# Decode rows and decode values as float32 matmuls on four column groups, and the 32-to-64 step of the inverse on packed odd columns, in one hybrid decoder layer

## The chip, the cores and the metric

The kernel runs on one core of a Trainium2 chip. A core has TensorE (PE, with its weight loads listed apart as PEld), VectorE (DVE), ScalarE (ACT), GpSimd (POOL) and SyncE (SP), which here issues all DMAs. The metric is device microseconds of one execution.

## The reference, cut to what matters

One layer serves 2048 prompt rows and 8 decode rows (one new token for each of 8 sequences) with the same weights: a mixer (a width-31 convolution module beside a gated DeltaNet with 4 heads), memory cross-attention, and a SwiGLU FFN.

```python
def gated_delta_chunked(q, k, v, g, beta, s0):        # chunks; per chunk:
    lower = jnp.where(strict, einsum(kb, k) * decay, 0.0)
    a_mat = lower + jnp.eye(c)
    u = triangular_solve(a_mat, v * beta[..., None])  # the kernel forms the inverse of a_mat
    w = triangular_solve(a_mat, kb * exp(gc)[..., None])

def memory_attend(h, mem_k, mem_v, w_mq, w_mo):
    q = (h @ w_mq).reshape(bsz, seq, MEM_HEADS, MEM_HD)
    pr = softmax(einsum('blhd,bmhd->bhlm', q, mem_k) * MEM_HD ** -0.5)
    o = einsum('bhlm,bmhd->blhd', pr, mem_v)
    return o.reshape(bsz, seq, MEM_HEADS * MEM_HD) @ w_mo

def decoder_layer(x, ...):
    x = x + parallel_mixer(rms_norm(x, norm_mix), ...)
    x = x + memory_attend(rms_norm(x, norm_mem_q), mem_k, mem_v, w_mq, w_mo)
    x = x + swiglu(rms_norm(x, norm_ffn), w_gate, w_up, w_down)
```

The decode rows have their own keys and values in a cache: 8 x 256 tokens x 1024 numbers each.

## The kernel before, in words

The prompt is cut into four blocks of 512 columns (TB). Big products use float32r operands, each split into a high part (ScalarE, rounded) and a low part (VectorE or GpSimd, the remainder); a product is then three matmuls: high x high, low x high, high x low (`three`). A float32 operand needs no split, but one call on it leaves two matmul records in the trace.

The program is written as one main line, which feeds TensorE, and many lanes (generators) that the main line advances by `tick`; a lane waits with `yield` for a tile, for room in a pool, for a PSUM bank, or for a time. Everything goes on a tape, and `Tape.order` then lists the instructions of each engine: it walks a model of the five engines, takes the ready instruction that stood earliest on the tape, and gives out tile buffers as it goes. So a change of durations or buffers anywhere places instructions anew behind it.

**The decode rows in the attention.** In the FFN of block 0, from f = 13, the main line takes the 16 row tiles of w_mq one after the other, two for each f; in the FFN of block 1, from f = 12, those of w_mo (`DEC_Q`, `DEC_O`, steps "dec" of `ffn_steps` and `ffn_steps_ds`). `dec_row` multiplies the 8 decode columns, as high and low parts side by side (16 columns of weights, tile hd_mix), by the high and the low part of a row tile of 128x512: two float32r matmuls into the tile dr. After eight tiles dr is copied, and the two halves are added by a matmul with the constant sel2 (tiles dq, dx).

Between the two lies the lane `dec_attend`: scores with the cached keys on VectorE, a softmax, and then the values. For each of two halves of the columns it loads 16 tiles of 128x512 (vtd; 8 sequences, 2 halves of the tokens), splits each (vth on ScalarE, vtl on VectorE), and multiplies by the packed probabilities (pb, 64 columns: 8 sequences x high and low x 4 heads) into the tile podd. `podt` is its transpose. The first row of w_mo needs the whole lane: there the main line calls `S.finish(dec_lanes["a"])`.

**The inverse.** `dn_front` runs 16 times (4 heads, 4 blocks) beside the projections, the attention products and the first FFN. A 128x128 matrix is inverted from 16x16 blocks upward, four matrices (NT) at a time: on the levels 16 and 32 a first product (pu from Tm with weights lo or lt), a mask (nms), a second product (pu from u1 with weights W), and a transpose of the inverse so far (ptw), copied to W. On level 16 the weights of the first product are the odd 16-blocks of lt, packed to 64 columns (lo), and W holds 64 rows. On level 32 they are the whole of lt and W. The last level, 64, is the same before and after.

Of the kernel before, what the change touches and what calls it, by code (L numbers as in the profile page):

```python
# [8 lines left out]
F32 = mybir.dt.float32  # L9
# [53 lines left out]
HOLD = 3  # L63
RES = 5
# [85 lines left out]
class Tape:  # L150
# [28 lines left out]
    def cost(self, eng, op, args, kw, outs, ins):  # L179
# [3 lines left out]
        if eng == "pe":  # L183
            m = elems(args[1])
            n = elems(args[2])
            if op == "transpose":
                return max(n, m) * 0.835 + 3, False, None
            if args[1].dtype == F32:
                return 2 * (max(max(m, 64) * 0.835, 2 * n * 0.4492) + 3), False, None
            return max(max(m, 64) * 0.835, (n if n >= 256 else 4 * n) * 0.4492) + 3, False, None  # L190
# [406 lines left out]
def hybrid_step(ctx: ExitStack, tc: tile.TileContext, i: dict, o: list):  # L597
# [23 lines left out]

    def transpose(out, in_, identity):
# [162 lines left out]
    def ffn_steps(b):  # L785
# [5 lines left out]
        for f in range(NF):  # L791
# [5 lines left out]
            dec = [w for w, (db, f0) in (("w_mq", DEC_Q), ("w_mo", DEC_O)) if db == b and f0 <= f < f0 + KC]  # L797
            steps += [("P5", f), ("P6", f)]
            steps += [("dec", dec[0], 2 * (f - (DEC_Q if dec[0] == "w_mq" else DEC_O)[1]) + n) for n in range(2) if dec]
            steps += [("Q2", f), ("Q3", f), ("Q7", f)]  # L800
            early = g is None and f + 1 < NF
# [5 lines left out]
            if g is not None:  # L807
                steps += [("down", g, j) for j in range(1, KC // 2)]
        if not hold and b != NB - 1:
            steps += [("down", NG - 1, j) for j in range(KC // 2)]  # L810
        return steps

    def ffn_steps_ds(b):
        steps = []
        for f in range(NF):
            if f == 0 or not early:
                steps.append(("Q1", f))
            dec = [w for w, (db, f0) in (("w_mq", DEC_Q), ("w_mo", DEC_O)) if db == b and f0 <= f < f0 + KC]
            steps += [("P5", f), ("P6", f)]
            steps += [("dec", dec[0], 2 * (f - (DEC_Q if dec[0] == "w_mq" else DEC_O)[1]) + n) for n in range(2) if dec]  # L820
# [6 lines left out]
            early = not units[0] + units[1] and f + 1 < NF  # L827
            if early:
                steps.append(("Q1", f + 1))
            steps += units[0] + [("P4", f)] + units[1]  # L830
# [26 lines left out]
    def ffn_plan(b):  # L857
        at = {}
        for st, f, *j in ffn_steps(b):
# [4 lines left out]
            elif st == "dec":  # L864
                plan.append((f, "r", j[0] % KC, j[0] // KC * TB))
# [85 lines left out]
    class WS:  # L951
# [60 lines left out]
        def split(self):  # L1012
            j = self.sp
            k = plan.raw_of[j]
            t = wpool.tile([P, 2, TB], F32R, tag="w", name=nm("w"))
# [6 lines left out]
            r = self.raw[k]  # L1022
# [296 lines left out]
    hd_mix = const("hd_mix", [P, KC, 16], F32R)  # L1319
# [7 lines left out]
    def dec_start():  # L1327
        dma(xd, i["xsT"])
        yield xd
        yield from dec_norm("norm_mix", hdn)  # L1330
        dec_split(hdn, hd_mix)
# [4 lines left out]
        for kc in range(KC):  # L1336
            mm(pb_, hd_mix[:, kc, 0:DEC], wbd[:, kc, :], kc == 0, False)
            mm(pb_, hd_mix[:, kc, DEC:16], wbd[:, kc, :], False, kc == KC - 1)
        V.tensor_copy(out=bd_dec, in_=pb_)
# [266 lines left out]
    def conv_block(b):  # L1606
# [4 lines left out]
        for t in range(NT):  # L1611
            sl = slice(b * TB + t * P, b * TB + (t + 1) * P)
            yield ("t2", 3 + RES)
# [22 lines left out]
            y = t2("lny", (P, 4, P))  # L1636
            for ct in range(4):
                A.activation(
                    out=y[:, ct, :], in_=pt[:, ct * P : (ct + 1) * P], func=AF.Silu, scale=vcol("conv_ln_g", ct),
                    bias=vcol("conv_ln_b", ct),  # L1640
                )
            dma(catc[:, :, sl].rearrange("c p t -> p c t"), y)
            drop(xi, x, y)
# [96 lines left out]

    def dn_front(h, b, sc, prev, out):
# [70 lines left out]
        dma(z_full(zl[z]), lt)  # L1812
        x16 = small("x16", [32, 272])
        w16 = small("w16", [32, 272], bufs=1)
# [11 lines left out]

        yield from base_inverse(x16, w16, bit)
# [6 lines left out]
        drop(bit, du)  # L1834
        W = t2("W", (64, NT, P))
# [7 lines left out]

        lo = small("lo", [P, NT, 64], bufs=1)
# [4 lines left out]
        for s in LEV[:-1]:  # L1849
            n = nms[s].shape[0]  # L1850
            yield ("ps", "s")
            pu = ps("pu1", shape=(n, NT, 64))
            for c in range(NT):
                mm(pu[:, c, :], (lo if n == 64 else lt)[:, c, :], left(Tm, s)[:, c], True, True)
            V.tensor_tensor(out=u1[:n], in0=pu, in1=bc(nms[s], 1, [n, NT, 64]), op=ALU.mult)
# [3 lines left out]
            for c in range(NT):  # L1859
                mm(pu[:, c, :], W[:, c, :], u1[:n, c, :], True, True)  # L1860
# [7 lines left out]
            W = t2("W", (P, NT, P))  # L1868
            A.activation(out=W, in_=pt, func=AF.Copy)
            yield W  # L1870

        yield ("ps", "s")
# [164 lines left out]
    for s, n_ in ((16, 64), (32, P)):  # L2037
        m = const(f"nms{s}", [n_, 64])
        GS.memset(m, -1.0)
        nb, w_ = 64 // s, n_ // 64 * s  # L2040
        GS.affine_select(out=m, in_=m, compare_op=ALU.is_ge, fill=0.0, base=s - w_, pattern=[[-w_, nb], [0, s]], channel_multiplier=1)
        GS.affine_select(out=m, in_=m, compare_op=ALU.is_ge, fill=0.0, base=w_ - 1, pattern=[[w_, nb], [0, s]], channel_multiplier=-1)
# [271 lines left out]
    def square_gemm(w, src, order, xs, done, dec, apart):  # L2314
# [10 lines left out]
        for m in range(n0):  # L2325
            if m == n0 - 1:
                S.until(lambda: any(C.bank_free(t) < 1e12 for t in ("mm", *others())), "fourth bank")
            pts.append([pm("rg", (P, hi - lo), others() if len(spans) * m + k > 2 else []) for k, (lo, hi) in enumerate(spans)])
# [27 lines left out]
    sel2 = const("sel2", [16, DEC])  # L2356
    V.tensor_tensor(out=sel2, in0=ident[:16, 0:DEC], in1=ident[:16, DEC:16], op=ALU.add)

    def dec_row(w, n, hd, then, at=[]):

        hf, kc = n // KC, n % KC
        if kc == 0:
            S.until(lambda: not any(c[0] is not None for c in convs) and C.bank_free("cv") < 1e12, "bank")
            at[:] = [ps("dr", "cv", (16, TB))]
        wt = ws.get(w, "r", kc, hf * TB)
# [3 lines left out]
        ws.free(1)  # L2369
        if kc == KC - 1:  # L2370
# [700 lines left out]
```

## Time and profile before

| | us |
|---|---|
| median of three runs | 2953.32 |
| lowest, highest | 2949.38, 2954.25 |
| profiled execution, span from first to last instruction | 2954.1 |
| mean granted TensorE clock | 0.995 |

The time of the profiled execution around its span isn't shown; the span lies within the three runs. By the first and last starts of their tiles, the input projections run to 711 us with the convolution and DeltaNet beside them and after them, the memory keys and values follow from 711, and the FFN of block 0 starts at 1175. The fronts end at 1452; the rows of w_mq stand from 1435 to 1562, the values from 1732 to 1947, the rows of w_mo from 1950 to 2052.

In the profile a row of a group gives line, engine, operation, tiles written<-read, sizes, count, then busy time, mean duration in ns, and idle time of the engine before it with what ended it. Nearly all instructions have line 474, a helper, so groups are told by their tiles. In the timeline, runs of like matmuls are merged to one row with a count; a bracket at its end is the idle time before it.

### The profile page before, as it was taken

The page shows a single profiled execution, that of the slowest core. Times are in us where ns is not written, and L with a number is a line of the kernel's source. Part 1 is how long each engine was busy: PE and PEld are TensorE (multiplying, and loading weights), DVE is VectorE, ACT ScalarE, POOL GpSimd, SP SyncE. Part 2 cuts the span into 40 slices and gives each one's busy share as a digit, 9 for nine tenths or more (in the row PEclk, how much of TensorE's full clock was granted, in tenths as well). Part 3 has the DMA queues.
Part 4 walks back from the last instruction along what each step waited for, and adds up shares of the span by engine and source line. Part 5 has one row for each costly group of instructions (what it writes and reads, how often), then busy time and mean ns, then how long its engine had stood idle before and what let it go on. Part 6 is the DMA issues. An engine that isn't in the chain of part 4 may idle for free.

```text
span 2954.1 us, 56406 instructions
## 1 busy us (share of the span) xinstructions
PE 2905.5 (98%) x19620; PEld 2619.1 (89%) x19620; DVE 2192.2 (74%) x4335; ACT 1486.5 (50%) x3093; POOL 1834.7 (62%) x1935
## 2 busy tenths in 40 slices
PE   9999999999999999999999999999999999999998
PEld 7999878887788888898988889989889999999998
DVE  8757888989655937977788976777865666776666
ACT  7544555555664545545554454444544444444444
POOL 4554454786546455558785138868514888758887
PEclk9999999999999999999999999999999999999999
DMA  6533335777673425755777677786627666666763
GB/s 215 154 101 111 125 106 166 239 255 239 203 257 110 144 86 186 224 184 184 257 241 257 221 239 221 227 257 217 195 86 228 205 207 181 211 230 194 215 207 124
DMA packets 363037, 569.44 MB, mean 193 GB/s; under 512 B 55840, under 2 KB 158560, under 8 KB 362736
## 3 DMA queue, kind: packets, MB, share of 16 engines
q1 hardware_dynamic: 362752, 565.84, 60.3%
q8 instruction: 155, 2.54, 0.4%
q14 instruction: 130, 1.06, 0.1%
HBM read 457.77 MB, written 108.51 MB: 192 GB/s over the span
## 4 chain that ended last, share of the span: by engine, by line
PE 85%; DVE 6%; DMA 4%; ACT 2%; POOL 2%; issue 1%; SPq 0%; POOLq 0%; DVEq 0%; ACTq 0%
PE fy L474 12%; PE rg L474 11%; PE hd L474 9%; PE fz L474 8%; PE fx L474 8%; PE sc L474 6%; PE dn L474 6%; PE dx L474 5%; PE dz L474 3%; PE glub L474 3%; PE glua L474 3%; PE pu L474 2%; DMA w<-sums 1%; DVE cacc L474 1%; PE dy L474 1%
## 5 line engine op out<-in xcount | busy, mean ns | idle before, releaser
L474 POOL TENSOR_TENSOR w<-raw,w 128x512 fp32r<-128x512 f32 (+1 forms) x777 | 1040.7, 1349 | 569.6 <-ACT w L474 514.3
L474 ACT ACTIVATE w<-raw 128x512 fp32r<-128x512 f32 (+1 forms) x1098 | 666.4, 619 | 900.0 <-PE rg L474 99.7
L474 PE MATMUL fy<-op,w 128*128 128x256 f32 (+1 forms) x3168 | 439.1, 283 | 4.2 <-DVE ffs L474 1.5
L474 PEld LDWEIGHTS fy<-op,w 128*128 128x128 f32 x3168 | 402.6, 189 | 9.7 <-DVE ffs L474 2.6
L474 PE MATMUL hd<-hT,w 128*128 128x512 f32 (+2 forms) x1920 | 395.8, 356 | 1.0 <-ACT w L474 0.6
L474 DVE SCALAR_TENSOR_TENSOR cacc<-cu,cw,cacc 128x512 f32<-128x512 f32 x480 | 359.2, 748 | 16.5 <-ACT cacc L474 9.7
L474 DVE TENSOR_TENSOR w<-raw,w 128x512 fp32r<-128x512 f32 (+1 forms) x321 | 287.5, 900 | 89.1 <-ACT w L474 86.4
L474 PEld LDWEIGHTS hd<-hT,w 128*128 128x128 f32 x1920 | 302.2, 188 | 45.4 <-ACT w L474 1.4
L474 PE MATMUL fx<-op,w 128*128 128x256 f32 (+1 forms) x2112 | 296.0, 284 | 6.6 <-ACT ffs L474 4.8
L474 PE MATMUL fz<-op,w 128*128 128x256 f32 (+1 forms) x2112 | 291.2, 283 | 2.9 <-DMA w<-sums 2.5
L474 POOL TENSOR_TENSOR sqj<-sqj,sqj 128x512 f32<-128x512 f32 (+1 forms) x98 | 134.1, 1368 | 251.8 <-ACT sqj L474 249.5
L474 PEld LDWEIGHTS fx<-op,w 128*128 128x128 f32 x2112 | 271.7, 190 | 12.3 <-ACT ffs L474 5.4
L474 PEld LDWEIGHTS fz<-op,w 128*128 128x128 f32 x2112 | 267.3, 189 | 8.2 <-issue 4.3
L474 POOL TENSOR_TENSOR raw<-raw 128x128 f32<-128x128 f32 x336 | 201.1, 610 | 8.2 <-DMA raw<-in_w_down_dram 5.5
L474 PE MATMUL dx<-fo,w 128*128 128x256 f32 (+1 forms) x1344 | 197.3, 284 | 0.8 <-ACT w L474 0.7
L474 PE MATMUL rg<-pT,w 128*128 128x512 f32 x768 | 191.3, 400 | 0.2 <-ACT pT L474 0.2
L474 PE MATMUL dn<-ff,w 128*128 128x512 f32 (+2 forms) x960 | 189.4, 350 | 0.0
L474 PE MATMUL rg<-catS,w 128*128 128x512 f32 (+2 forms) x960 | 188.2, 352 | 0.0
L474 PE MATMUL sc<-w,hT 128*128 128x512 f32 x768 | 186.5, 398 | 0.0
L474 PEld LDWEIGHTS dx<-fo,w 128*128 128x128 f32 x1344 | 174.2, 188 | 4.3 <-ACT w L474 0.9
L474 PEld LDWEIGHTS rg<-catS,w 128*128 128x128 f32 x960 | 154.4, 188 | 24.2
L474 POOL TENSOR_TENSOR raw<-raw,raw 128x128 f32<-128x128 f32 (+1 forms) x179 | 164.1, 919 | 17.0 <-DVE w L474 8.4
(404 smaller groups left out, 5123.4 us busy)
## 6 DMA issues: line engine op xcount, KB each, us to landing
w<-sums SPq DMA_DIRECT2D x222, 512.0 KB, 4.3
raw<-in_w_gate_dram SPq DMA_DIRECT2D x192, 256.0 KB, 3.3
sums<-w SPq DMA_DIRECT2D x66, 512.0 KB, 4.0
raw<-in_w_up_dram SPq DMA_DIRECT2D x118, 256.0 KB, 3.7
raw<-in_w_down_dram SPq DMA_DIRECT2D x224, 128.0 KB, 2.6
raw<-in_w_in_dram SPq DMA_DIRECT2D x96, 256.0 KB, 3.4
raw<-sums SPq DMA_DIRECT2D x74, 256.0 KB, 3.2
raw<-wk SPq DMA_DIRECT2D x64, 256.0 KB, 2.8
```

The source lines that it names most:

```text
L474: fn(*args, **kw)
```

## The change

The decode rows: `dec_rows` replaces `dec_row`. Four row tiles of w_mq or w_mo are taken raw, without a split, and multiplied as float32 by the 8 float32 decode columns, each of the four into its own 32 partitions of the tile dr (`quad`: column groups 0, 32, 64, 96), in two rounds for each half. This stands at four places (every second f, behind the product P4) in place of sixteen. The four groups are copied apart into a cleared tile and added by sel2, now with 128 rows.

The decode values: a batch is four raw tiles (two sequences, two halves of the tokens), multiplied as float32 by 32 columns of probabilities each, in the four column groups of podd; the lane then yields `VPACE` (10 us of the planner's time). No vth, no vtl.

The inverse: on level 32 the weights are the odd 32-blocks of lt, packed to 64 columns in the same tile lo by one more copy on ScalarE; W of that level has 64 rows, being the transpose of the odd 32-blocks of Tm (packed by a second copy, tile to). Three locks (held_x, held_w, held_l) let a lane wait for the buffers x16, w16 and lo.

Smaller: hd_mix is no longer a constant tile but a temporary one in `dec_start`; the layer norm of the convolution writes over its input tile; `square_gemm` asks for a bank only where it takes one outside the first three.

```diff
+    def quad(out, j, lhsT, rhs, start, stop):
+        m = elems(lhsT)
+        out = out[32 * j : 32 * j + m]
+        S.wait(max(C.when([lhsT, rhs]), C.ready.get("free " + out.name, 0.0) if start else 0.0))
+        PE.matmul(out, lhsT, rhs, start=start, stop=stop, skip_group_check=True)
+        C.run("pe", 15 + elems(rhs) / 2.2, [lhsT, rhs], out, 90.0)
...
-            early = g is None and f + 1 < NF
+            early = g is None and f + 1 < NF and not dec
...
+            steps += [("dec", *x) for x in dec]
...
-                plan.append((f, "r", j[0] % KC, j[0] // KC * TB))
+                plan.extend((f, "f", j[0] % 2 * 4 + n, j[0] // 2 * TB) for n in range(4))
...
         for s in LEV[:-1]:
-            n = nms[s].shape[0]
             yield ("ps", "s")
-            pu = ps("pu1", shape=(n, NT, 64))
+            pu = ps("pu1", shape=(64, NT, 64))
             for c in range(NT):
-                mm(pu[:, c, :], (lo if n == 64 else lt)[:, c, :], left(Tm, s)[:, c], True, True)
+                mm(pu[:, c, :], lo[:, c, :], left(Tm, s)[:, c], True, True)
+            if s == 16:
+                A.activation(out=lo.rearrange("p c (b s) -> p c b s", s=32), in_=left(lt, 32, 1), func=AF.Copy)
...
+            n, to = P, Tm
+            if s == 16:
+                n, to = 64, small("to", [P, NT, 64], bufs=1)
+                A.activation(out=to.rearrange("p c (b s) -> p c b s", s=32), in_=left(Tm, 32, 1), func=AF.Copy)
+                yield to
             yield ("ps", "s")
-            pt = ps("ptw", shape=(P, NT, P))
+            pt = ps("ptw", shape=(n, NT, P))
             for c in range(NT):
-                transpose(pt[:, c, :], Tm[:, c, :], ident)
+                transpose(pt[:, c, :], to[:, c, :], ident)
...
-        mm(at[0], hd[:, kc, :], wt[:, 0, :], kc == 0, False)
-        mm(at[0], hd[:, kc, :], wt[:, 1, :], False, kc == KC - 1)
+        wts = [ws.get(w, "f", k0 + j, hf * TB) for j in range(4)]
+        for j in range(4):
+            quad(at[0], j, h[:, k0 + j, :], wts[j], k0 == 0, k0 == 4)
...
-                    A.activation(out=vh, in_=vt, func=AF.Copy)
-                    yield vh
-                    V.tensor_tensor(out=vl, in0=vt, in1=vh.bitcast(F32), op=ALU.subtract)
-                    yield pbs + [vl]
-                    pb = pbs[mc][:, b * 64 : (b + 1) * 64]
-                    mm(po, pb, vh, b == 0 and mc == 0, False)
-                    mm(po, pb, vl, False, b == DEC - 1 and mc == 1)
+                for (d, mc), vt in vts.items():
+                    quad(po, 2 * d + mc, pbs[mc][:, (b + d) * 32 : (b + d + 1) * 32], vt, b == 0, b == DEC - 2)
+                drop(*vts.values())
+                yield VPACE
```

Three places of TensorE's order follow (line, operation, tiles with buffer numbers, sizes, count).

The decode values just ahead of the first row of w_mo, before: the end of the second half stands in one block.

```order
L474 MATMUL fy_4467<-op_3989,w_4451 128x256 x3
L474 MATMUL podd_4385<-vtl_4406,pb_3949 64x512
L474 MATMUL podd_4385<-vth_4408,pb_3950 64x512
L474 MATMUL podd_4385<-vtl_4409,pb_3950 64x512
L474 MATMUL podd_4385<-vth_4411,pb_3949 64x512
L474 MATMUL podd_4385<-vtl_4412,pb_3949 64x512
L474 MATMUL podd_4385<-vth_4414,pb_3950 64x512
L474 MATMUL podd_4385<-vtl_4415,pb_3950 64x512
L474 MATMUL podd_4385<-vth_4417,pb_3949 64x512
L474 MATMUL podd_4385<-vtl_4418,pb_3949 64x512
L474 MATMUL podd_4385<-vth_4420,pb_3950 64x512
```

Now, in the middle of the first half, some 500 rows ahead of the first row of w_mo:

```order
L479 MATMUL podd_3991<-vtd_4052,pb_3935 32x512
L479 MATMUL podd_3991<-vtd_4053,pb_3936 32x512
L479 MATMUL fx_4060<-op_3948,w_4057 128x256 x3
L479 MATMUL fx_4060<-op_3955,w_4057 128x256 x3
L479 MATMUL fx_4060<-op_3965,w_4057 128x256 x3
L479 MATMUL fx_4060<-op_3974,w_4057 128x256 x3
L479 MATMUL podd_3991<-vtd_4090,pb_3935 32x512
L479 MATMUL fz_4067<-op_3949,w_4054 128x256 x3
L479 MATMUL fz_4067<-op_3956,w_4054 128x256 x3
L479 MATMUL fz_4067<-op_3966,w_4054 128x256 x3
L479 MATMUL fz_4067<-op_3975,w_4054 128x256 x3
L479 MATMUL podd_3991<-vtd_4091,pb_3936 32x512
```

The block is gone, the last value stands at row 4732 and the first matmul of w_mo at row 4978 of TensorE's 7677, and a batch of four is at places cut into twos and single matmuls.

The decode rows of w_mo (tile dr), before eight in a row:

```order
L474 MATMUL dx_4481<-fo_4363,w_4468 128x256 x3
L474 MATMUL dx_4481<-fo_4399,w_4471 128x256 x3
L474 MATMUL dr_4448<-w_4375,hd_mix 16x512 x2
L474 MATMUL dr_4448<-w_4378,hd_mix 16x512 x2
L474 MATMUL dr_4448<-w_4453,hd_mix 16x512 x2
L474 MATMUL dr_4448<-w_4455,hd_mix 16x512 x2
L474 MATMUL dz_4483<-fo_4362,w_4472 128x256 x3
```

Now the second round of the same half, from raw tiles:

```order
L479 MATMUL fy_4467<-op_3976,w_4454 128x256 x3
L479 MATMUL dr_4409<-raw_4433,hcat 8x512
L479 MATMUL dr_4409<-raw_4435,hcat 8x512
L479 MATMUL dr_4409<-raw_4436,hcat 8x512
L479 MATMUL fy_4467<-op_3950,w_4461 128x256 x3
L479 MATMUL fy_4467<-op_3957,w_4461 128x256 x3
L479 MATMUL fy_4467<-op_3967,w_4461 128x256 x3
L479 MATMUL fy_4467<-op_3976,w_4461 128x256 x3
L479 MATMUL dr_4409<-raw_4443,hcat 8x512
L479 MATMUL fx_4482<-op_3947,w_4470 128x256 x6
```

Half as many matmuls, of 8 columns in place of 16; this round is cut into three and one.

Level 32 of the inverse, before (the last front: transpose of level 16, first product, second product):

```order
L474 MATMUL fy_3346<-op_2652,w_3386 128x256
L474 MATMUL ptw_3367<-ident,Tm_3335 128x128 x4
L474 MATMUL pu_3172_3371<-Tm_3335,lt_3213 128x64 x4
L474 MATMUL lnq_3383<-ident,lnx_3380 128x128 x4
L474 MATMUL fy_3346<-op_2652,w_3386 128x256 x2
L474 MATMUL fy_3346<-op_2660,w_3386 128x256 x3
L474 MATMUL fy_3346<-op_2670,w_3386 128x256 x3
L474 MATMUL po_3389<-S_3349,dn_3208 128x128
L474 MATMUL fy_3346<-op_2681,w_3386 128x256
L474 MATMUL pu_3174_3373<-u_218,W_3368 128x64 x4
```

Now (a front in the projections, the same three steps):

```order
L479 MATMUL ptw_1011<-ident,to_1003 64x128 x4
L479 MATMUL hd_983<-hT_1042,w_853 128x512
L479 MATMUL hd_1134<-hT_1042,w_855 128x512
L479 MATMUL po_985<-chv_1010,at_754 128x128
L479 MATMUL pch_1004<-chv_1010,kd_752 128x128
L479 MATMUL pu_826_1023<-Tm_954,lo_989 64x64 x4
L479 MATMUL hd_983<-hT_1042,w_853 128x512
L479 MATMUL pch_1031<-S_1021,kT_746 128x128
L479 MATMUL po_985<-S_1021,rb_751 128x128
L479 MATMUL hd_983<-hT_1042,w_853 128x512
L479 MATMUL hd_983<-hT_1045,w_853 128x512
L479 MATMUL pu_836_1033<-u_217,W_1012 128x64 x4
```

The first product takes lo in place of lt and writes 64 partitions; the transpose takes to and writes 64; the second product looks the same here, but its weights W now have 64 rows.

More of the change, by code (lines that the diff above doesn't have):

```diff
@@ L63 @@
 HOLD = 3
+VPACE = 10000.0
 RES = 5
@@ L187, in cost @@
                 return max(n, m) * 0.835 + 3, False, None
+            if args[1].dtype == F32 and m <= 32 and n >= 256:
+                return n * 0.4492 + 15, False, None
             if args[1].dtype == F32:
@@ L817, in ffn_steps_ds @@
                 steps.append(("Q1", f))
-            dec = [w for w, (db, f0) in (("w_mq", DEC_Q), ("w_mo", DEC_O)) if db == b and f0 <= f < f0 + KC]
+            dec = [(w, (f - f0) // 2) for w, (db, f0) in (("w_mq", DEC_Q), ("w_mo", DEC_O)) if db == b and f0 <= f < f0 + KC and (f - f0) % 2]
             steps += [("P5", f), ("P6", f)]
-            steps += [("dec", dec[0], 2 * (f - (DEC_Q if dec[0] == "w_mq" else DEC_O)[1]) + n) for n in range(2) if dec]
             steps += [("Q2", f), ("Q3", f), ("Q7", f)]
@@ L1014, in split @@
             k = plan.raw_of[j]
+            r = self.raw.get(k)
+            if plan[j][1] == "f":
+                self.tiles[j] = r
+                self.sp += 1
+                return
             t = wpool.tile([P, 2, TB], F32R, tag="w", name=nm("w"))
@@ L1825, in dn_front @@
         yield x16
+        yield lambda: not held_w
+        held_w.append(1)
+        w16 = small("w16", [32, 272], bufs=1)
         yield from base_inverse(x16, w16, bit)
@@ L1842, in dn_front @@
         u1 = u1s[0]
+        yield lambda: not held_l
+        held_l.append(1)
         lo = small("lo", [P, NT, 64], bufs=1)
@@ L2435, in dec_attend @@
         yield ("t2", 2)
-        pbs = [t2("pb", dt=F32R) for _ in range(2)]
+        pbs = [t2("pb", (P, DEC * 32)) for _ in range(2)]
         yield ("ps", "s")
@@ L2475, in dec_attend @@
             yield ("ps", "s")
-            pt = ps("podt", shape=(P, 4, 64))
+            pt = ps("podt", shape=(P, 4, P))
             for k in range(4):
-                transpose(pt[:, k, :], pr[:, k * P : (k + 1) * P], ident[:64, :64])
+                transpose(pt[:, k, :], pr[:, k * P : (k + 1) * P], ident)
             for k in range(4):
-                own = pt[:, k, :].rearrange("p (b l h) -> p b l h", l=2, h=MH)[:, :, :, 2 * hf + k // 2]
-                V.tensor_reduce(out=od[:, hf * 4 + k, :], in_=own, op=ALU.add, axis=AX.X)
+                own = pt[:, k, :].rearrange("p (d m i e h) -> p d e h i m", d=2, m=2, e=2, h=MH)
+                to = od[:, hf * 4 + k, :].rearrange("p (i e) -> p e i", e=2)
+                for d in range(2):
+                    V.tensor_reduce(out=to[:, d, :], in_=own[:, d, d, 2 * hf + k // 2], op=ALU.add, axis=AX.X)
             drop(pr)
```

118 lines of the change are left out of this document (59 added, 59 removed).

## The prediction

> **What bounds the kernel now.** I read the page's busy table first, then the chain that ended last, then TensorE's waits, and only then the stretches that the change touches.
>
> ```profile
> span 2954.1 us, 56406 instructions
> PE 2905.5 (98%) x19620; PEld 2619.1 (89%) x19620; DVE 2192.2 (74%) x4335; ACT 1486.5 (50%) x3093; POOL 1834.7 (62%) x1935
> PE 85%; DVE 6%; DMA 4%; ACT 2%; POOL 2%; issue 1%; SPq 0%; POOLq 0%; DVEq 0%; ACTq 0%
> ```
>
> TensorE is busy for 98% of the span and holds 85% of the chain. What another engine saves is worth nothing unless TensorE waits for it just there. So each edit is priced by two things: how long the matmuls that it adds or removes occupy TensorE, and whether it ends a wait of TensorE. A matmul's own duration is no use for the first, because matmuls are pipelined: I take the distance from the start of one row of the timeline to the start of the next (columns: start, length, engine, line, operation, tiles, sizes, count).
>
> **Decode matmuls before.** These rows come from the decode values (podd) and the decode rows (dr), all float32r.
>
> ```profile
> 1896.84 0.86 PE L474 MATMUL dz<-fo,w 128*128 128x256 f32 x6
> 1897.54 0.40 PE L474 MATMUL podd<-vth,pb 128*64 128x512 f32 x1
> 1897.77 0.40 PE L474 MATMUL podd<-vtl,pb 128*64 128x512 f32 x1
> 1898.01 0.88 PE L474 MATMUL dx<-fo,w 128*128 128x256 f32 x6
> ...
> 1950.20 2.02 PE L474 MATMUL dr<-w,hd_mix 128*16 128x512 f32 x8
> 1952.05 0.87 PE L474 MATMUL dz<-fo,w 128*128 128x256 f32 x6
> ```
>
> The podd matmuls start 0.23 apart and the eight dr take 1.85, 0.231 each. Nothing is lost on entering or leaving: six dz before podd take 0.70, 0.117 each, and dx starts 0.24 after the last podd. There are 64 dr and 64 podd:
>
> ```profile
> L474 PE MATMUL dr<-w,hd_mix x64: 387/396/478, 1435.3 to 2051.4; 128*16 128x512 f32 x64
> L474 PE MATMUL podd<-vth,pb x32: 387/392/628, 1732.4 to 1946.3; 128*64 128x512 f32 x32
> L474 PE MATMUL podd<-vtl,pb x32: 388/394/628, 1732.7 to 1947.0; 128*64 128x512 f32 x32
> ```
>
> 128 x 0.232 = 29.7 us.
>
> **Decode matmuls after.** 64 float32 matmuls on column groups of 32. The nearest thing in the trace is dq, a float32 matmul with 8 columns of weights over 512 columns; it is called twice, and each call leaves two matmul records.
>
> ```profile
> L474 PE MATMUL dq<-dr,sel x4: 587/589/592, 1496.5 to 1562.8; 16*8 16x512 f32 x4
> 1496.04 0.52 PE L474 MATMUL fz<-op,w 128*128 128x256 f32 x3
> 1496.49 1.02 PE L474 MATMUL dq<-dr,sel 16*8 16x512 f32 x2
> 1497.44 1.34 PE L474 MATMUL fz<-op,w 128*128 128x256 f32 x9
> ```
>
> The two passes together last 1.02 and one lasts 0.59, so the second starts 0.43 after the first. Three fz at 0.118 end at 1496.39, the next full matmul starts at 1497.44: one call costs 1.05, of which 0.86 are its two passes and 0.19 is lost on entering and leaving. The Trainium skill (TensorEngine Tiling (Array Packing), Key Properties) says that changing the tiling mode drains TensorE. The dq rows agree (0.19); the podd rows, also of less than 128 columns but float32r, show no such loss. If the rule held for them too, the 53 places where dr or podd stand in before's order would have paid 53 x 0.19 = 10 us that the change saves, and the sum would be -18; the rows say that they don't, and I follow them.
>
> How much four neighbours overlap, no row of before shows. One bound is full overlap: an uninterrupted piece of up to four costs 1.05. The other is none: 0.86 for each matmul and 0.19 for each piece. In the new order of TensorE the 64 stand in 24 pieces (11 of four, one of three, five of two, seven alone), because the four values of a batch are placed as their loads are expected. Full overlap: 24 x 1.05 = 25.2. None: 64 x 0.86 + 24 x 0.19 = 59.6. I take the end near full overlap, because the four write separate quarters of the partitions, use separate columns of the array and don't depend on each other; to it I add 1.0 us for the 40 further matmuls of the pieces (0.025 each, a choice that no row prices). **26.2 - 29.7 = -3.5 us**, with -4.5 and +29.9 as ends.
>
> **The inverse.** There are 16 fronts (head and block). On the level from 32 to 64 the first product (pu<-Tm) goes from 128 columns of weights to 64, and the second (pu<-u,W) from 128 rows to 64. The level from 16 to 32 already has both new forms, so all four prices stand in the trace:
>
> ```profile
> 153.70 0.52 PE L474 MATMUL hd<-hT,w 128*128 128x264 f32 x3
> 154.06 1.00 PE L474 MATMUL pu<-Tm,lt 128*128 128x64 f32 x8
> 154.87 0.61 PE L474 MATMUL hd<-hT,w 128*128 128x256 f32 x3
> ...
> 199.69 0.88 PE L474 MATMUL hd<-hT,w 128*128 128x256 f32 x6
> 200.41 1.00 PE L474 MATMUL pu<-u,W 128*128 128x64 f32 x8
> 201.21 0.49 PE L474 MATMUL hd<-hT,w 128*128 128x256 f32 x2
> ...
> 217.19 0.65 PE L474 MATMUL glub<-hT,w 128*128 128x256 f32 x4
> 217.76 0.68 PE L474 MATMUL pu<-Tm,lo 128*64 128x64 f32 x8
> 218.37 0.51 PE L474 MATMUL glub<-hT,w 128*128 128x256 f32 x2
> 220.81 0.39 PE L474 MATMUL po<-chv,dn 128*128 128x128 f32 x2
> 221.03 0.39 PE L474 MATMUL pch<-chv,dn 128*128 128x128 f32 x2
> 221.35 1.10 PE L474 MATMUL pu<-u,W 64*128 64x64 f32 x8
> 222.38 0.50 PE L474 MATMUL glua<-hT,w 128*128 128x512 f32 x1
> ```
>
> Before: 0.81 and 0.80, and entering costs nothing (three hd of 0.12 fill 0.36). After, first product: 0.61, and four glub that need 0.47 fill 0.57, so 0.10 more for entering: 0.71, a gain of 0.10. After, second product: 1.03, and two pch fill 0.32 where two po fill 0.22, so 0.10 more: 1.13, a loss of 0.33. Sixteen fronts: 16 x (0.33 - 0.10) = **+3.7 us**. The smaller product is the dearer one here, since its cover of full-size neighbours is lost. The halved transpose (ptw) saves nothing, for the time goes by the 128 columns that stream and not by the columns that are kept:
>
> ```profile
> 150.26 0.66 PE L474 MATMUL ptw<-ident,Tm 128*128 128x128 f32 x4
> 150.75 0.38 PE L474 MATMUL pq<-ident,qTd 128*128 128x128 f32 x2
> ...
> 1698.55 0.38 PE L474 MATMUL psc<-ident,scs 128*32 128x128 f32 x2
> 1698.77 1.04 PE L474 MATMUL ppt<-ident,pr 128*128 128x128 f32 x8
> ```
>
> Four full ones take 0.49, two of 32 columns 0.22: 0.11 or 0.12 each in both; the bounds are 0 and a gain of half, 16 x 0.24 = 3.8, and I take 0 after the psc row. ScalarE gets two copies of 128x256 more in each front, about 32 x 0.41 = 13 us by the row of lo below, and loses the 32 splits of values and 32 of rows; it is 50% busy, and TensorE has the input projections to do meanwhile. If that cover were gone, one more hop of about 0.4 on each front would cost up to 16 x 0.4 = 7 us; the copies of the second lo stand behind no wait of TensorE.
>
> ```profile
> L474 ACT ACTIVATE lo<-lt 128x256 f32<-128x256 f32 x16 | 6.6, 412 | 7.8 <-DVE lt L474 5.9 <-PE pu L474 1.9
> ```
>
> **The splits of the values.** VectorE loses 32 vtl, 30.5 us in all. Off TensorE's path that is nothing, but not everywhere:
>
> ```profile
> 1929.00:1937.00 8.00, 4.28 (x17) 1.67 (x17) 5.36 (x7) 2.81 (x6) 6.78 (x8) 1.00 0.83 248
> 1937.00:1942.00 5.00, 5.00 (x24) 4.22 (x22) 2.77 (x4) 2.94 (x5) 0.84 (x1) 0.66 0.50 188
> 1921.00:1950.00 29.00, 23.95 (x147) 19.05 (x146) 22.54 (x39) 13.95 (x25) 14.73 (x15) 0.94 0.76 248
> 1921.00:1950.00 29.00, 9.98 (x29) 3.62 (x29) 0.59 (x1) 0.94 0.76 248
> 1927.04 4.92 DVE L474 TENSOR_TENSOR vtl<-vtd,vth 128x512 fp32r<-128x512 f32 x4
> ```
>
> The first two rows (stretch, length, busy time and count of TensorE, its weight loads, VectorE, ScalarE, GpSimd, then granted clock and DMA) show a hole: the first row of w_mo must have the decode attention, what is left of its values is forced through VectorE (last row: four vtl in 4.92), and TensorE idles for almost half of 8 us and then runs 5 us at a clock of 0.66. The third row is the whole stretch, with 147 matmuls, the fourth podd's share, 29. The other 118 need 118 x 0.118 = 13.9 us and the 29 need 6.7, together 20.6 of 29: 8.4 us are lost. After, nothing is split, a batch of four needs its loads only, and in the new order some 250 rows of TensorE stand between the last value and the first matmul of w_mo. I count the hole as gone: **-8.4 us**, the lower bound; the upper is 0, the hole comes back elsewhere. Next late there would be the loads of the values:
>
> ```profile
> DMA to landing us min/median/max: 2.8/5.1/6.8
> ```
>
> Median 5.1 us from issue to landing, against batches 10 us apart.
>
> **Sum.** -3.5 + 3.7 - 8.4 = -8.2. The profiled span of 2954.1 would be 2945.9. Its time outside the span isn't shown; the three runs lie from 2949.4 to 2954.3 with a median of 2953.3, so I take the same 8.2 off the median: **2945.1 us**. The 32 splits of weight rows that go, the memsets of dr and its 16 small copies lie beside TensorE's work and count as nothing.
>
> **Rivals.** (1) *Column groups wait in line* (slower). A float32 call is two passes on the same columns. If matmuls start in program order, the second pass of group 0 waits 0.43 for its own columns, and group 1 stands behind it: only the second pass of one and the first of the next overlap. A piece of k then costs (k + 1) x 0.43 + 0.19; over 24 pieces 88 x 0.43 + 24 x 0.19 = 42.4, which is +12.7 in place of -3.5, so 2953.3 + 8.0 = 2961.3. It decides from pieces that take over 1.4 us on average, where the three terms cancel (29.7 + 4.7 over 24). For it: dq's passes stand 0.43 apart. Against it: no row shows whether a different group is held up. The Trainium skill (TensorE: Matmul & The Clock Gate, The mechanism) says that matmuls start and end strictly in program order, and that tiles on other columns run together; the first sentence gives this rival, the second my forecast, and no run here shows either for two column groups. (2) *No overlap at all*: +29.9 + 3.7 - 8.4 = +25.2, 2978.5. Against it speaks only that the groups are independent. (3) *The change doesn't free the hole*: the batches are spaced by 10 us, eight of them need 80 us at least, and a pair of matmuls on late loads blocks TensorE as vtl did. Then -3.5 + 3.7: 2953.5. Against it: the 5.1 us of a load and the 250 rows of room. (4) *The fronts wait longer* for the extra ScalarE copies: up to +7 on the forecast, 2952.
>
> **How the numbers follow.** Overlap with the hole gone 0.65, waiting in line 0.2, no overlap 0.07, the hole stays or fronts wait 0.08. All instructions behind the change are placed anew, and TensorE's waits sum to 48.6 us (span less busy), so each case gets some 6 us on both sides. Within 0.2% (5.9 us, about what a measurement here can tell): the first case then gives faster 0.40, same 0.24, the second same 0.06 and slower 0.13, the third slower 0.07, the fourth same 0.05. Rounded: faster 0.43, same 0.33, slower 0.24. The range takes in the first case to 10 us below and the second to 5 above: 2935 to 2966; the likeliest case alone spans 2937 to 2953.
>
> **What would show it.** Right: four dr or podd calls in a row fill about 1.1 us from start to next start; pu with 64 rows of weights stands 32 times at 1.03; no idle of TensorE between the last podd and the first dr of w_mo, and a clock of 1.00 there. Wrong: such a piece fills 2.3 (in line) or 3.6 (no overlap); a new wait for loads of raw or vtd; longer waits on Tm and W between 100 and 1450 us.

## The result and the profile after

The changed kernel takes 2963.95 us (median of 17 runs, 2960.52 to 2972.53), the kernel before 2956.34 in 17 runs beside it (2949.38 to 2963.33). The ratio is 1.0029, 95% interval 1.0021 to 1.0038: 0.29% slower, some 8.6 us by the ratio and 7.6 by the medians, where 8.2 us less were forecast.

The page after, span, busy time of each engine, and the shares of the chain that ended last:

```profile
span 2966.1 us, 56231 instructions
...
PE 2910.1 (98%) x19620; PEld 2602.6 (88%) x19620; DVE 2139.8 (72%) x4265; ACT 1466.3 (49%) x3067; POOL 1830.1 (62%) x1949
...
PE 83%; DVE 6%; DMA 4%; POOL 3%; issue 2%; ACT 1%; SPq 0%; POOLq 0%; DVEq 0%; ACTq 0%
```

VectorE and ScalarE have less to do, as the change meant, and TensorE is the bound as before. Its idle time (span less busy) grew from 48.6 to 56.0 us, and GpSimd's share of the chain from 2% to 3%.

Where the 12.0 us of the two profiled spans come from is read at two points that the change leaves alone: the scores of the memory attention (tile sc, 192 matmuls for each block), which TensorE does in one piece. The tile's rows for the third and fourth block, first before, then after (count, duration, first and last start):

```profile
L474 PE MATMUL sc<-w,hT x192: 388/394/496, 1646.4 to 1692.6; 128*128 128x512 f32 x192
...
L474 PE MATMUL sc<-w,hT x192: 387/394/496, 2160.7 to 2208.0; 128*128 128x512 f32 x192
```

```profile
L479 PE MATMUL sc<-w,hT x192: 387/394/497, 1658.6 to 1704.9; 128*128 128x512 f32 x192
...
L479 PE MATMUL sc<-w,hT x192: 388/394/502, 2170.8 to 2218.0; 128*128 128x512 f32 x192
```

The first stretch ends 12.2 us later. The second, which holds the values, the hole and the rows of w_mo, is 512.2 in place of 514.3 us, a gain of 2.1 where some 11 were forecast (the hole, 8.4, and 2.6 of the quads). The third is 795.3 in place of 793.4. So two things need a cause: a loss of 12 us in the first stretch, where the prediction had some 3 (the inverse, less the rows of w_mq), and 9 us of the gain in the second that didn't come.

**The three terms in the trace.** The decode matmuls, in TensorE's timeline after (start, length, operation, tiles, sizes, count):

```profile
1482.78 1.08 PE L479 MATMUL dn<-ff,w 128*128 128x512 f32 x4
1483.79 1.04 PE L479 MATMUL dr<-raw,hdn 128*8 128x512 f32 x8
1484.76 1.68 PE L479 MATMUL fx<-op,w 128*128 128x256 f32 x12
...
1778.70 1.56 PE L479 MATMUL fy<-op,w 128*128 128x256 f32 x12
1780.19 1.05 PE L479 MATMUL podd<-vtd,pb 128*32 128x512 f32 x4
1781.17 1.11 PE L479 MATMUL fx<-op,w 128*128 128x256 f32 x7
```

Four dr calls (eight records) fill 0.97 us, two podd calls (four records) fill 0.98, and a call of dr alone at 1998.42 fills 0.96: the four groups overlap in full, and a piece costs the same whether one, two or four calls stand in it. Rivals 1 and 2 would have been 2.3 and 3.6.

The inverse on the new forms:

```profile
307.03 0.86 PE L479 MATMUL glub<-hT,w 128*128 128x512 f32 x3
307.82 0.68 PE L479 MATMUL pu<-Tm,lo 128*64 128x64 f32 x8
308.43 0.97 PE L479 MATMUL glub<-hT,w 128*128 128x512 f32 x3
...
314.29 0.86 PE L479 MATMUL glua<-hT,w 128*128 128x512 f32 x3
315.08 1.10 PE L479 MATMUL pu<-u,W 64*128 64x64 f32 x8
316.11 0.66 PE L479 MATMUL pvv<-ident,vT 128*128 128x128 f32 x4
```

0.61 and 1.03 from start to next start, and three full matmuls that need 0.70 fill 0.79 ahead of either: the prices of the prediction. The hole (stretch, length, TensorE's, its weight loads', VectorE's, ScalarE's and GpSimd's busy time, clock, DMA), from behind the last value to ahead of the rows of w_mo, and then the place where the second loss sits, after and, in the last row, before:

```profile
1880.00:1962.00 82.00, 81.10 (x675) 80.29 (x676) 51.78 (x107) 35.73 (x71) 64.95 (x73) 1.00 0.69 224
2060.00:2080.00 20.00, 13.29 (x108) 12.75 (x105) 13.77 (x19) 7.02 (x13) 10.82 (x19) 0.83 0.57 193
...
2060.00:2080.00 20.00, 17.98 (x137) 17.61 (x136) 15.37 (x22) 11.64 (x23) 16.53 (x19) 0.91 0.63 200
```

The hole is gone: 0.9 us idle in 82, clock 1.00. But 20 us at 2060 now hold 6.7 us of idle time and a clock of 0.83, another 3.4 us; before, they held 2.0 us of idle time and a clock of 0.91, 1.8 us. So the place costs some 6.3 us more than before. TensorE's waits (waited for, us in total, times, longest) name the tile, and the timeline of VectorE and GpSimd shows it:

```profile
PE dnb L479 <- DVE tbd L479: 5.9, 1, 5.9
PE pss L479 <- DVE sqj L479: 3.6, 2, 2.8
PE fz L479 <- DMA w<-sums: 3.3, 6, 1.5
```

```profile
2067.86 1.00 POOL L479 TENSOR_TENSOR tbr<-tbm,ex 8x1 f32<-8x1 f32 x1
...
2068.84 1.26 POOL L479 TENSOR_TENSOR w<-raw,w 128x512 fp32r<-128x512 f32 x1
2068.90 6.17 DVE L479 TENSOR_SCALAR tbd<-ident,tbr 8x8 f32<-8x8 f32 x1
...
2070.07 0.85 POOL L479 TENSOR_TENSOR raw<-raw 128x128 f32<-128x128 f32 x2
...
2074.59 0.44 POOL L479 TENSOR_TENSOR raw<-raw 128x128 f32<-128x128 f32 x1
2074.99 0.41 DVE L479 TENSOR_TENSOR ffs<-ffu,ffs 128x256 f32<-128x256 f32 x1
```

tbd is an 8x8 product of the decode norm that stands behind the rows of w_mo (norm_ffn). It took 0.42 us before (2056.18) and takes 6.17 now: it starts 0.06 behind the first of thirteen GpSimd instructions that follow each other without a pause (a split and the sums of w_down) and ends when they do.

### The profile page after: what moved, and what is told of

It reads as the page before. It is cut to its first block, busy times and chain, and to the rows that moved or that the text cites. A ratio compares the mean times of both kernels' runs of the same rounds, so it can differ in the third digit from the quotient of the medians.

```text
span 2966.1 us, 56231 instructions
## 1 busy us (share of the span) xinstructions
PE 2910.1 (98%) x19620; PEld 2602.6 (88%) x19620; DVE 2139.8 (72%) x4265; ACT 1466.3 (49%) x3067; POOL 1830.1 (62%) x1949
## 4 chain that ended last, share of the span: by engine, by line
PE 83%; DVE 6%; DMA 4%; POOL 3%; issue 2%; ACT 1%; SPq 0%; POOLq 0%; DVEq 0%; ACTq 0%
PE fy L479 11%; PE hd L479 11%; PE rg L479 9%; PE fz L479 7%; PE fx L479 7%; PE sc L479 6%; PE dn L479 5%; PE dx L479 5%; PE glub L479 3%; PE dz L479 2%; PE glua L479 2%; PE pu L479 2%; DMA w<-sums 2%; DVE cacc L479 2%; PE pch L479 1%
## 5 line engine op out<-in xcount | busy, mean ns | idle before, releaser
L479 ACT ACTIVATE w<-raw 128x512 fp32r<-128x512 f32 (+1 forms) x1066 | 647.4, 619 | 859.3 <-PE dx L479 100.4
L479 DVE TENSOR_TENSOR w<-raw,w 128x512 fp32r<-128x512 f32 (+1 forms) x281 | 245.2, 877 | 87.5 <-ACT w L479 82.6
L479 POOL TENSOR_TENSOR raw<-raw 128x128 f32<-128x128 f32 x336 | 189.7, 576 | 24.6 <-DMA raw<-in_w_down_dram 21.9
```

What stands on the lines that cost most here:

```text
L479: fn(*args, **kw)
```

## The experiments

Theory: the prediction's terms hold, and the loss is in waits of TensorE that came with the new order. Rivals: the inverse's new step, or the decode part, has a price of its own that the prediction lacks. All ratios are to the kernel before, run beside it on the same chip. The columns on stretches are differences to before in the profiled executions (before: 1646.4, 514.3, 793.4); five kernels whose TensorE order is the same in the first stretch (after, e4, e5, e6, e12) differ by 2 us there, which is the noise of one execution.

| kernel | ratio, 95% interval | to the third sc | to the fourth | to the end |
|---|---|---|---|---|
| after | 1.0029 (1.0021, 1.0038) | +12.2 | -2.1 | +1.9 |
| e1 decode only | 1.0021 (1.0011, 1.0031) | +9.3 | +1.3 | -1.1 |
| e2 inverse only | 1.0045 (1.0033, 1.0058) | +17.6 | -3.9 | -2.1 |
| e3 locks and norm only | 1.0017 (1.0007, 1.0027) | +6.6 | -0.9 | -2.1 |
| e4 tbd, two inputs | 1.0035 (1.0023, 1.0046) | +10.2 | -3.1 | -0.4 |
| e5 sums on VectorE | 1.0018 (1.0009, 1.0027) | +10.2 | -5.0 | +0.2 |
| e6 tbd on ScalarE | 1.0041 (1.0027, 1.0055) | +11.5 | -1.8 | -0.2 |
| e7 before, placed anew | 1.0065 (1.0052, 1.0077) | +15.8 | +5.4 | -2.1 |
| e8 after, placed anew | 1.0054 (1.0042, 1.0067) | +17.8 | -3.7 | -1.3 |
| e9 values only | 0.9962 (0.9949, 0.9975) | +1.0 | -8.0 | -2.7 |
| e10 before, placed anew, 2 | 1.0053 (1.0039, 1.0067) | +11.7 | +2.7 | -2.4 |
| e11 after, placed anew, 2 | 1.0031 (1.0020, 1.0041) | +12.8 | -1.8 | +0.1 |
| e12 rows early | 1.0024 (1.0013, 1.0036) | +11.9 | -3.5 | -0.8 |

**e1, the decode part alone** (against the changed kernel; locks and layer norm are also those of before):

```diff
-            if s == 16:
-                n, to = 64, small("to", [P, NT, 64], bufs=1)
-                A.activation(out=to.rearrange("p c (b s) -> p c b s", s=32), in_=left(Tm, 32, 1), func=AF.Copy)
...
-                mm(pu[:, c, :], lo[:, c, :], left(Tm, s)[:, c], True, True)
+                mm(pu[:, c, :], (lo if n == 64 else lt)[:, c, :], left(Tm, s)[:, c], True, True)
```

> The kernel before with the decode rows and values of the changed kernel (raw tiles on four column groups, temporary hd_mix) and the old inverse, with none of the locks and the old layer norm buffers. Theory (the prediction's terms are right in size, the loss is in waits of TensorE that the new placement brings, above all the 5.9 us for tbd at 2069 and those of the fronts between 400 and 1600): the two decode terms alone are -3.5 and -8.4, so -12 against the kernel before if no new wait of some size comes, a ratio of about 0.996; the tiles dr and podd take 26 to 27 us in all. Rival A (the inverse's new step carries the loss of 10 us before 1601 us): also -12. Rival B (the decode part carries it, since four raw tiles and the temporary hd_mix take buffers from the fronts and loads): 0 to +6, with TensorE some 10 us late at 1600 us.

2960.43 against 2954.86 us, slower by 0.21%, where the theory had 12 us less: a miss. Rival A falls too: without the new inverse, 9.3 us are lost before the third sc. The tile tbd lasts 6.18 us here too, at 2069.13. Rival B's numbers fit, but not yet its cause.

**e2, the inverse alone** (against before):

```diff
+            if s == 16:
+                n, to = 64, small("to", [P, NT, 64], bufs=1)
+                A.activation(out=to.rearrange("p c (b s) -> p c b s", s=32), in_=left(Tm, 32, 1), func=AF.Copy)
+                yield to
...
+                transpose(pt[:, c, :], to[:, c, :], ident)
```

> The kernel before with the new step from 32 to 64 of the inverse and its three locks, decode and layer norm as before (the constants of two decode steps that never overlap share a buffer, to make room for the tile to). Theory: +3.7 by the prediction's prices, so a ratio of 1.001, and on top what placement does, which can have either sign by some 4 us; the hole at 1921 to 1950 is there as before. Rival A (the two copies on ScalarE lengthen every front and the inverse carries the loss): +10 to +12, a ratio of 1.0035 to 1.004, with TensorE 10 us late by 1600 us and longer waits on Tm, W and u. Rival B (the decode part carries it): +4 or less.

2968.16 us, slower by 0.45%, all of it in the first stretch. The number, 13.3 us by the medians, is nearest to rival A's and too large for the theory. But e1 and e2 together would then make the changed kernel 0.66% slower, and it is 0.29%: the two don't add, which fits placement and no price by parts.

**e3, the locks and the layer norm alone** (against before):

```diff
+        yield lambda: len(held_x) < 2
+        held_x.append(1)
...
-            y = t2("lny", (P, 4, P))
-                    out=y[:, ct, :], in_=pt[:, ct * P : (ct + 1) * P], func=AF.Silu, scale=vcol("conv_ln_g", ct),
+                    out=xi[:, ct, :], in_=pt[:, ct * P : (ct + 1) * P], func=AF.Silu, scale=vcol("conv_ln_g", ct),
```

> The kernel before with the locks held_x and held_w, the later allocation of w16 and the layer norm that writes over its input tile; the inverse's products and the decode part are those of before. No instruction is added or taken away but for the tiles it uses. Theory (placement): no term of its own; whatever differs from the kernel before is placement, within 4 us either way. Rival C (the locks hold fronts back, or the reused layer norm tile delays the convolution): +5 to +8, with TensorE late by that much at 1200 us.

2960.44 us, slower by 0.17%, with no instruction more; in its profile TensorE is 6.6 us late at the third sc. That is rival C's size; whether the locks do it or the new order was left to e7.

**e4, tbd in another form** (against the changed kernel, for the last decode norm only):

```diff
-        V.tensor_scalar(out=dg[:n, :n], in0=ident[:n, :n], scalar1=r[:n, :], scalar2=None, op0=ALU.mult)
+        V.tensor_tensor(out=dg[:n, :n], in0=ident[:n, :n], in1=r[:n, :].to_broadcast([n, n]), op=ALU.mult)
```

> The changed kernel with one instruction in another form: the 8x8 product tbd of the last decode norm (ident times a scalar for each row) as a TENSOR_TENSOR with the scalar broadcast, in place of the TENSOR_SCALAR that lasted 6.17 us at 2068.9 while GpSimd ran without a pause. TensorE's order is the same to the last row. Theory: the TENSOR_SCALAR gets no access while GpSimd's instructions follow each other; the other form takes under 1 us, the 5.9 us wait goes and so does most of the half clock (6.8 us at 0.5, 3.4 lost) behind it: -6 to -9 against the changed kernel, a ratio to the kernel before of 0.9995 to 1.0005. Rival (something else holds VectorE there, a semaphore or the scalar's write): the new form lasts 6 us too, no change. Rival (the wait is only handed on: VectorE's next instruction is held instead and TensorE waits for ffu or fo): 0 to -2.

VectorE's row in e4:

```profile
2065.17 6.16 DVE L479 TENSOR_TENSOR tbd<-ident,tbr 8x8 f32<-8x8 f32 x1
```

The theory about the form was wrong: 6.16 us again, no change of the time. Either GpSimd's run holds any such instruction, or tbd waits for something else.

**e5, the sums moved to VectorE** (against the changed kernel):

```diff
-            eng = self.engine(2600.0)
+            eng = V if at in ((7, 2), (6, 3), (7, 3)) else self.engine(2600.0)
```

> The changed kernel, but three sets of sums of w_down (four 128x128 additions each) that GpSimd did in one run from 2070 to 2075 us, while tbd waited, are given to VectorE; TensorE's order is the same up to 2010 us and differs little behind it. e4 has shown that tbd lasts 6.16 us in either form. Theory (VectorE's instruction gets its turn only when GpSimd pauses): tbd takes under 1.5 us, the wait of 5.9 us for it goes, the half clock behind it goes: -6 to -9 against the changed kernel, a ratio to before of 0.9995 to 1.0005. Rival (tbd's delay has another cause, as the scalar written by GpSimd): tbd lasts 6 us again and nothing changes. Rival (handed on: VectorE falls behind by its 12 further additions of some 0.25 us and TensorE waits for ffs or ffu): -1 to -4.

tbd lasts 1.22 us, so GpSimd's run was its cause. TensorE still waits 2.3 us for it, as VectorE comes to it later, and the ratio is 1.0018 for 1.0029 of the changed kernel: -3 us, within the overlap of the two intervals, the size of the last rival.

**e6, tbd on ScalarE** (against the changed kernel, for the last decode norm only):

```diff
-        V.tensor_scalar(out=dg[:n, :n], in0=ident[:n, :n], scalar1=r[:n, :], scalar2=None, op0=ALU.mult)
+        A.activation(out=dg[:n, :n], in_=ident[:n, :n], func=AF.Copy, scale=r[:n, :])
```

> The changed kernel with the 8x8 product tbd of the last decode norm on ScalarE (activation with a scale for each row); GpSimd's run of sums stays, TensorE's order is the same to the last row. Theory (GpSimd's run starves every VectorE instruction that reads two inputs or is of this kind, whichever comes next): tbd takes under 0.5 us and dnb waits no more, but VectorE's next instruction (ffs) lasts 5 us or more in its place, ScalarE's fo waits for it, its ffu behind it, and TensorE waits 3 to 6 us at the next fx: 0 to -3. Rival (only an instruction that reads what GpSimd has just written is held): no VectorE instruction over 2 us there, and -6 to -9.

VectorE's and ScalarE's rows, and the wait of TensorE at this place:

```profile
2068.48 6.51 DVE L479 TENSOR_TENSOR ffs<-ffu,ffs 128x256 f32<-128x256 f32 x1
...
2068.55 0.30 ACT L479 ACTIVATE tbd<-ident,tbr 8x8 f32<-8x8 f32 x1 [0.33 <-POOL tbr L479]
...
2075.90 2.93 PE L479 MATMUL fx<-op,w 128*128 128x256 f32 x12 [6.44 <-ACT ffu L479]
```

As expected by the theory: tbd is done in 0.30, the next instruction of VectorE is held for 6.51 in its place, and TensorE waits 6.4 us for what hangs on it. It is this run of GpSimd that holds VectorE, whatever stands next. The time doesn't fall: the ratio is 1.0041 for 1.0029, where 0 to 3 us less were expected, though the two intervals overlap.

**e7 and e10, the kernel before placed anew; e8 and e11, the changed kernel with the same edits** (e7 and e8 with 2200, e10 and e11 with 1800):

```diff
-SLACK = 2000.0
+SLACK = 2200.0
```

> The kernel before with one constant of the planner's clock (the head start that lanes get) raised by a tenth: no instruction is added or removed, but most rows of TensorE from 30 us on stand in another order. Theory (the prediction's three terms hold, the loss is what placement anew brings, and the placement of before is a favourable one): +3 to +8, a ratio of 1.001 to 1.003, in waits of TensorE of 1 to 3 us at other places and more half clock. Rival (placement anew is neutral on average and e1 to e3 each have a price of their own): within 2.5 us of before.

> The changed kernel with the same constant raised by a tenth. Theory (placement): within 6 us of the changed kernel either way (2958 to 2970), since its placement is one draw among others; if the constant leaves the starved tbd behind, at the lower end. Against e7 it shows what the change does where both are placed anew: by the prediction's terms -8 or with the wait for tbd 0. Rival (the change has a price of its own in the fronts and loads that any placement pays): 7 us or more above e7.

> The kernel before with the planner's constant of e7 lowered by a tenth in place of raised; most rows of TensorE behind 30 us stand in another order. Theory (before's placement is a favourable draw): +3 to +20, since e7 gave +19.8 and e3 +5.6. Rival (e7 was an unlucky draw): within 3 us of before.

> The changed kernel with the planner's constant lowered by a tenth. Theory (the change itself is worth -8, or about 0 where tbd is starved, and placement adds its own draw): below e10 or at most 4 us above it; with e7 and e8 (2972.9 and 2969.5) the mean difference of the two pairs lies between -10 and +2. Rival (the change has a price of its own that any placement pays): 7 us or more above e10.

The kernel before, with no instruction added or removed, is 0.65% and 0.53% slower (2972.90 and 2971.69 us, beside 2953.08 and 2955.03). The direction is the theory's; the 19.8 us of e7 are far above its 3 to 8. The stretch up to 1640 us, with the columns of the hole's rows; first before, then after, then e7:

```profile
0.00:1640.00 1640.00, 1614.90 (x10001) 1398.36 (x10002) 1267.81 (x2484) 886.24 (x1916) 967.59 (x1015) 1.00 0.58 185
```

```profile
0.00:1640.00 1640.00, 1609.72 (x9948) 1382.13 (x9949) 1245.50 (x2445) 883.26 (x1927) 972.05 (x1022) 1.00 0.57 182
```

```profile
0.00:1640.00 1640.00, 1608.24 (x9933) 1390.62 (x9933) 1255.72 (x2462) 870.99 (x1892) 965.37 (x1013) 0.99 0.56 182
```

TensorE is idle for 25.1 us of it before, 30.3 after, 31.8 in e7, which holds no part of the change. Placed anew with the same constant, the changed kernel is the faster one both times: 2969.51 against 2972.90, and 2965.23 against 2971.69, by 3.4 and 6.5 us. The intervals of each pair's ratios overlap, so no single pair proves the sign; the rival of e8 and e11 (7 us or more above) lies far from both.

**e9, the values alone** (against before; every engine's order is that of before up to 1690 us):

```diff
-                    A.activation(out=vh, in_=vt, func=AF.Copy)
-                    yield vh
-                    V.tensor_tensor(out=vl, in0=vt, in1=vh.bitcast(F32), op=ALU.subtract)
...
-                    mm(po, pb, vh, b == 0 and mc == 0, False)
-                    mm(po, pb, vl, False, b == DEC - 1 and mc == 1)
+                for (d, mc), vt in vts.items():
+                    quad(po, 2 * d + mc, pbs[mc][:, (b + d) * 32 : (b + d + 1) * 32], vt, b == 0, b == DEC - 2)
+                drop(*vts.values())
+                yield VPACE
```

> The kernel before with the decode values alone changed (raw tiles on four column groups, batches of four, no splits); decode rows, inverse, locks and layer norm are those of before, and every engine's order is that of before up to 1690 us. Theory (the prediction's terms hold; the loss is placement of what lies before 1690 and the starved tbd at 2069): nothing is lost up to 1690, the hole at 1921 to 1950 goes (-8.4, the prediction's figure) and the values cost half of the quads' term (16 batches for 32 x 2 matmuls, about -1.5): -7 to -11 against before, a ratio of 0.9963 to 0.9976, if no new wait comes behind 1950. Rival (the hole only moves: what is late there is another thing, as the loads): -2 to +2, with idle time of TensorE of 4 us or more between 1730 and 2110 as before.

2945.75 us (2941.28 to 2946.15) against 2955.03: faster by 0.38%, as the theory had it, and faster than both kernels. The two tile rows of sc:

```profile
L479 PE MATMUL sc<-w,hT x192: 388/394/499, 1647.4 to 1693.6; 128*128 128x512 f32 x192
...
L479 PE MATMUL sc<-w,hT x192: 387/394/499, 2153.7 to 2200.9; 128*128 128x512 f32 x192
```

With the old order ahead of it nothing is lost in the first stretch, and the second gains 8.0 us.

**e12, the rows of w_mo at their old place** (against the changed kernel):

```diff
-            steps += [("P5", f), ("P6", f)]
+            steps += [("P5", f), ("P6", f)] + [("dec", *x) for x in dec]
...
-            steps += units[0] + [("P4", f)] + units[1] + [("dec", *x) for x in dec]
+            steps += units[0] + [("P4", f)] + units[1]
```

> The changed kernel with the decode rows of w_mo back at their old place in the step of the FFN, between P6 and Q2 in place of behind P4 and the w_down products; nothing else, and TensorE's order is the same up to 1950 us. In all four kernels with the rows at the new place tbd lasted 6.16 to 6.18 us, in all with the old rows 0.42. Theory (the move of the rows put the decode norm beside GpSimd's unbroken run of sums): tbd takes under 1.5 us, the 5.9 us wait goes, idle time of TensorE between 1960 and 2110 falls from 7.4 to 3 or 4 and some half clock with it: -4 to -7 against the changed kernel, a ratio to before of 1.0005 to 1.0015. Rival (the raw loads or the four-tile batches bring it there wherever the rows stand): tbd lasts over 5 us again, within 2 us of the changed kernel.

VectorE's row, and the head of TensorE's waits in e12:

```profile
2065.50 0.21 DVE L479 TENSOR_SCALAR tbd<-ident,tbr 8x8 f32<-8x8 f32 x1
```

```profile
PE fx L479 <- ACT ffs L479: 5.7, 4, 3.1
```

The mechanism is right: tbd takes 0.21 us, the wait for dnb is gone. The size is a miss: the ratio is 1.0024 for 1.0029, since a wait of 3.1 us for ffs has come in its place. So the wait of 5.9 us is worth some 1 to 3 us when it is taken away (e5, e12), not the 6 to 9 or 4 to 7 that were expected.

## Why the prediction was wrong

**The quads: right.** 1.05 for a piece of one call and some 1.1 for one of four were forecast; 0.96 to 0.98 and 0.07 to enter (four dn that need 0.94 fill 1.01) were measured. Rivals 1 and 2 didn't happen.

**The inverse: right as far as TensorE's own prices go** (0.61 and 1.03, and 0.09 to enter). Whether its two copies on ScalarE lengthen the fronts (rival 4) can't be told from the times: e2 loses 17.6 us in the first stretch, but e7 loses 15.8 there with none of it. The sign that the prediction named for it, longer waits of TensorE on Tm and W, didn't come; before and after:

```profile
PE pu L474 <- DMA Tm<-zt: 5.7, 4, 3.2
...
PE pu L479 <- DMA Tm<-zt: 1.8, 1, 1.8
PE pu L479 <- ACT W L479: 0.9, 1, 0.9
```

**The hole: right in kind, priced somewhat high.** It is gone after, and e9, which has little else, gains 8.0 us in its stretch and 9.3 by the medians, the values' matmuls with it. Idle time (29 less 23.95) and clock (0.94) of the 29 us before make 6.8 us, not 8.4.

**The step that failed** is this one: "All instructions behind the change are placed anew, and TensorE's waits sum to 48.6 us (span less busy), so each case gets some 6 us on both sides." Placement was taken as noise around zero. It is one-sided here: the order of before is a good one in the first stretch, and the two kernels that only place it anew are later at the third sc by 15.8 (e7) and 11.7 us (e10); e3, which adds no instruction, by 6.6. All orders tried there that differ from before's are later, by 6.6 to 17.8; the changed kernel by 12.2. Of these, 5.2 are idle time (25.1 to 30.3), in many waits of up to some 2 us, and 3.4 are clock: up to the third sc the clock is granted at 0.50 for 13.7 us in the profile after and for 6.8 in that of before. The longest piece of each, after and before (TensorE's busy time, clock, DMA):

```profile
424.00:435.00 11.00, 9.05 (x48) 0.69 0.31 89
...
800.00:811.00 11.00, 7.76 (x39) 0.69 0.62 205
```

The rest, 3.6 us, is TensorE's work at the full clock, near the 2.8 that were forecast for this stretch (the inverse's 3.7, less 0.9 for the rows of w_mq); it wasn't split by tile. In e3 TensorE is idle no longer than before (24.7), and its loss is the clock (20.5 us at 0.50). Idle time and lost clock together are 28.5 us in this stretch before and 32.1 in e9, which has the same order of TensorE there; they are 34.9 to 38.1 in the five kernels with the changed kernel's order and 34.9 to 45.9 in the seven others, each from one profile. The chance of slower thus belonged on the forecast case itself, since the change replaces the order from the first front on.

**A step that was left out:** the prediction followed the moved rows of w_mo to TensorE, but not the decode norm behind them. In all four kernels that have the rows at the new place and tbd in its old form and engine, with GpSimd's sums left alone (after, e1, e8, e11), tbd lasts 6.16 to 6.18 us; in all with the rows at the old place (before, e2, e3, e7, e9, e10) it lasts 0.42, and in e12 0.21. That is an effect of the change and no draw of placement. It lies in the second stretch, where the changed kernel gains 2.1 us and e9 8.0; e5 gives 2.9 us of that back, and e12 1.4.

So the sum of -8.2 was not given back by the three terms: e9 keeps its gain. Against the forecast, some 9 us were lost to the new order of the first 1640 us and some 9 in the second stretch, there mostly at the decode norm (6.3 us more of idle time and clock than before) and by the hole that was priced 1.6 too high. No rival of the prediction had either. That the time still lies inside 2935 to 2966 is luck: the upper end was set for column groups that wait in line, and they don't. Which choices of the planner give before's order fewer waits and less half clock than the others stays open.

## What to carry to other kernels

Where a scheduler places everything anew, compare the change with the kernel before under two or three neutral edits of the scheduler, too: here these alone cost 17 and 20 us, more than any term. (Whether the value 2000 had been picked because its order is good isn't on record.) Apply a gain where it leaves the order ahead of it alone; the values alone gained 9 us, the whole change lost 8 to 9. When a step is moved, follow what stands behind it to its engine, and look at what the neighbour engine does there in one run.

## What the runs showed of the hardware

A VectorE instruction on a few numbers was held for 6.16 to 6.51 us by thirteen GpSimd instructions that followed each other without a pause, most of them only 0.41 apart, whether it was a TENSOR_SCALAR (6.17) or a TENSOR_TENSOR (6.16) of 8x8 or one of 128x256 (6.51, 0.41 where it isn't held). The Trainium skill (SBUF — State Buffer, Who interferes with whom) says that the two engines share a pair of ports as an exclusive lock that is held for the full instruction. The trace agrees that VectorE stands still, but here it does not come in between two GpSimd instructions: the hold lasts as long as the run. That isn't so in every such run. In the changed kernel GpSimd works without a pause from 1895.7 to 1901.5, too, and a VectorE instruction with two inputs takes 0.82 there (its median is 0.71), while two of GpSimd's additions take 1.32 in place of 0.85:

```profile
1897.76 1.32 POOL L479 TENSOR_TENSOR raw<-raw 128x128 f32<-128x128 f32 x2
...
1897.95 0.82 DVE L479 TENSOR_TENSOR ffu<-ffu,ffs 128x512 f32<-128x512 f32 x1
```

What decides which of the two engines is held isn't shown by these runs.

Calls of float32 on different column groups overlap in both of their passes: four fill 0.97 us, two 0.98, one 0.96.

Short waits go ahead of a halved clock here: a wait of 1.5 us and one of 0.8 at 423.6 and 427.0 in the changed kernel stand ahead of 6.8 us at 0.50, and one of 2.0 at 2066.9 in the kernel before ahead of 3.4 us. Not every wait does so: behind one of 2.0 at 826.9 in the kernel before the clock stays at 1.00.
